# A hybrid attention and delta-rule layer: the scan's output products issued as two column halves

## The chip, the cores and the metric

The kernel runs on one core of one Trainium2 chip. The metric is device time in microseconds (us), the median of the runs shown. A second source is one execution taken with the hardware profiler; its times within the span (from the first to the last instruction) are what the views of the profile give.

## The reference, cut to what matters

The layer takes 256 latent tokens and 256 context tokens of width 2048 and has two branches, multi-head latent attention and a gated DeltaNet with 8 heads, which are projected, gated, summed and followed by a gated MLP. The change lies in the DeltaNet's scan: tokens in chunks of 64, one scan forward and one backward (each with its own decay and gates), first over the four context chunks, whose outputs are not needed, then over the four latent chunks. One step of the reference, per head and direction:

```python
    def step(s, inp):
        u_c, w_c, k_c, g_c = inp[:4]
        v_new = u_c - jnp.einsum('bhcd,bhde->bhce', w_c, s)
        s_next = s * g_c + jnp.einsum('bhcd,bhce->bhde', k_c, v_new)
        if not with_out:
            return s_next, None
        q_c, a_c = inp[4:]
        o = jnp.einsum('bhcd,bhde->bhce', q_c, s) + jnp.einsum('bhcj,bhje->bhce', a_c, v_new)
        return s_next, o
```

The change concerns `o`: the state read by the queries, plus the chunk's attention applied to the new values. Channels are 128 per head.

## The kernel before, in words

Everything before and after the scan is large projections. Each weight matrix comes from memory as fp32 (`raw`, tiles of 128 x 1024, five buffers), is split into a rounded high part `whi` (ScalarE) and a rest `wlo` (VectorE), six buffers of 512 columns each, and TensorE multiplies both: `whi` with 512 moving columns (high and low part of the activations), `wlo` with 256. These are the `fps`, `dps`, `gtp`, `brp` and other groups of the profile; all of them are issued by a helper, so all TensorE rows have line L68 and are told apart by tile names. The weights are stationary: 128 x 128 at a time. A product of plain fp32 operands shows in the profile as two matmuls with a weight load each; here each of the two is called a pass.

The scan is a generator (`scan`, below). It goes through eight steps in the order `steps`, four of the context and then four of the latents (`lat`). Both directions are handled at once: the 64 tokens of the forward chunk lie on partitions 0 to 63 and those of the backward chunk on 64 to 127, and the state `S` has for each head a tile of 128 channels by 128 for each direction. A step does in turn:

- `kp` (from the second step on): keys by state, for each head and direction, into one half of the partitions of a PSUM tile (`kps[h // 4][hs, h % 4]`), so with 64 stationary columns; then VectorE makes the right-hand sides `r`.
- after a yield, `yp`: the solved triangular system by `r`; ScalarE copies it to `y`.
- after another yield, in latent steps, for the two halves `q` of four heads: the outputs `op` (changed here), and in all steps but the last the state update: `sp_`, keys by `y`, from one half of the rows per direction, added to `S` by VectorE (copied by ScalarE in the first step). In `op`, `y` (stationary) is multiplied with `av` for both directions at once, 128 moving columns; then for each direction `S` (stationary) with `qe`, 64 moving columns, is added. The 128 output channels lie on PSUM's partitions.
- ScalarE (steps with `st < 2`) or VectorE copies or adds `op` into `o`.

At each yield the loop around the scan lets a side generator (`fill`) issue projections, the gates `gtp` (`wgd`) and the attention branch's output `brp` (`womla`), and another (`ada`) issue reductions of a conditioning matrix (`rawa`, VectorE, L279). TensorE's order there is pinned to the order of the program; the order on VectorE, SP's DMA queue and the rest comes from a scheduler that weighs the costs of instructions.

The loads of a latent step, `av` (from `As`, L1247) and `qe` (L1249), go into single buffers, so they wait in SP's queue for the `op` of the step before, and loads queued behind them wait too.

Of the kernel before, what the change touches and what calls it, by code (L numbers as in the profile page):

```python
# [53 lines left out]
def hybrid_block(ctx: ExitStack, tc: tile.TileContext, io, dbg=None):  # L54
# [20 lines left out]
    pe, oact, odve = (Ordered(e) for e in (nc.tensor, nc.scalar, nc.vector))  # L75
# [4 lines left out]
    def pool_(name, bufs, side="left"):  # L80
        return tc.tile_pool(name=name, bufs=bufs, side=side, reuse_waits="tile")
# [402 lines left out]
    for k in range(KD):  # L484

        p, late = k // 2 + 1, k % 2 and k + 1 < KD and (k + 1) // 2 in SCP
# [726 lines left out]
    def scan():  # L1213
        pS = ExitStack()
        ps1 = pS.enter_context(pool_("scan", 1, "right"))
        jit = ps1.tile([P, 9, 1024], F32, name="jit")
        TTv = [jit[:, 6 + n].rearrange("p (h c) -> p h c", c=P) for n in range(3)]
        for n in range(3):
            pool.memset(jit[:, 6 + n], 0.0)
        S = ps1.tile([P, HEADS, 2, P], F32, name="S")  # L1220
        steps = (4, 5, 6, 7, 0, 1, 2, 3)

        def load_kv(n):
            kt, v = (jit[:, 2 * j + n % 2].rearrange("p (h c) -> p h c", c=P) for j in (0, 2))
            sync.dma_start(kt, KTs[steps[n]])
            sync.dma_start(v, Vs[steps[n]])
            return kt, v

        def load_system(n):
            st, tt = steps[n], TTv[n % 2]  # L1230
            for d in range(2):
                for r, c, x in ((0, 0, Xq[1]), (32, 32, Xq[2]), (0, 32, Xo)):
                    rs, cs = slice(64 * d + r, 64 * d + r + 32), slice(64 * d + c, 64 * d + c + 32)
                    n = 16 * d + 2 * st
                    sync.dma_start(tt[rs, :, cs], x[n : n + 2].rearrange("a g c i -> c (a g) i"))
            return tt

        def load_ke(n):
            ke = jit[:, 2 + n % 2].rearrange("p (h c) -> p h c", c=P)
            sync.dma_start(ke, KEs[steps[n]])  # L1240
            return ke

        def load_out(st):
            av = TTv[2]
            for d in range(2):
                hs = slice(64 * d, 64 * d + 64)
                sync.dma_start(av[hs, :, hs], As[st, hs])  # L1247
            qe = ps1.tile([P, HEADS, P], F32, tag="qe", name="qe")
            sync.dma_start(qe, QEs[st])  # L1249
            return av, qe  # L1250


        kv, tt, ke = load_kv(0), load_system(0), load_ke(0)
        yield 0
        for n, st in enumerate(steps):
            kt, v = kv
            lat, first, last = st < 4, n == 0, n == 7
            if lat:
                av, qe = load_out(st)
            if n and not last:  # L1260
                ke = load_ke(n)
            if first:
                rs = [v[:, 4 * q : 4 * q + 4] for q in range(2)]
            else:
                rs = [ps1.tile([P, 4, P], F32, tag="r", name="r", bufs=2) for _ in range(2)]
                kps = [psa.tile([P, 4, P], F32, tag="aux", name="kp") for _ in range(2)]

                for h in range(HEADS):
                    for d in range(2):
                        hs = slice(64 * d, 64 * d + 64)  # L1270
                        pe.matmul(kps[h // 4][hs, h % 4], kt[:, h, hs], S[:, h, d], start=True, stop=True)
                for h in range(HEADS):
                    dve.scalar_tensor_tensor(out=rs[h // 4][:, h % 4], in0=kps[h // 4][:, h % 4], scalar=negc[:, st, h : h + 1], in1=v[:, h], op0=ALU.mult, op1=ALU.add)
            if not last:
                kv = load_kv(n + 1)
            yield CA
            y = ps1.tile([P, HEADS, P], F32, tag="y", name="y")
            for q in range(2):
                h4 = slice(4 * q, 4 * q + 4)
                yp = psa.tile([P, 4, P], F32, tag="aux", name="yp")  # L1280
                for j in range(4):
                    pe.matmul(yp[:, j], tt[:, 4 * q + j], rs[q][:, j], start=True, stop=True)
                act.copy(y[:, h4], yp)
            if not last:
                tt = load_system(n + 1)
            yield CB
            if lat:
                op = [psm.tile([P, 4, 2, 64], F32, tag="mm", name="op") for q in range(2)]
            for q in range(2):
                h4 = slice(4 * q, 4 * q + 4)  # L1290
                if lat:
                    for j in range(4):
                        h = 4 * q + j
                        pe.matmul(op[q][:, j].rearrange("p d i -> p (d i)"), y[:, h], av[:, h], start=True, stop=False)
                        for d in range(2):
                            pe.matmul(op[q][:, j, d], S[:, h, d], qe[:, h, 64 * d : 64 * d + 64], start=False, stop=d == 1)
                if not last:
                    for d in range(2):
                        hs = slice(64 * d, 64 * d + 64)
                        sp = psa.tile([P, 4, P], F32, tag="aux", name="sp_")  # L1300
                        for j in range(4):
                            pe.matmul(sp[:, j], ke[hs, 4 * q + j], y[hs, 4 * q + j], start=True, stop=True)
                        if first:
                            act.copy(S[:, h4, d], sp)
                        else:
                            for j in range(4):
                                h = 4 * q + j
                                dve.scalar_tensor_tensor(out=S[:, h, d], in0=S[:, h, d], scalar=gend[:, d, st, h : h + 1],
                                                         in1=sp[:, j], op0=ALU.mult, op1=ALU.add)
            if lat:  # L1310
                for d in range(2):
                    c = st if d == 0 else 3 - st
                    for q in range(2):
                        dst = o[:, 4 * q : 4 * q + 4, 64 * c : 64 * c + 64]
                        src = op[q][:, :, d] if d == 0 else op[q][:, :, d, ::-1]
                        if st < 2:
                            act.copy(dst, src)
                        else:
                            dve.tensor_tensor(out=dst, in0=src, in1=dst, op=ALU.add)
            yield CC  # L1320
        pS.close()
# [36 lines left out]
    for c in scan():  # L1358
        fill(RE * c)
        ada(ADS * c)  # L1360
# [92 lines left out]
    for f in range(NFF):  # L1453
# [12 lines left out]
        y = pf2.tile([P, T], F32, tag="fy", name="fy")  # L1466
# [127 lines left out]
```

## Time and profile before

| what | us |
|---|---|
| runs of the kernel before: median (lowest to highest) of 3 | 1819.82 (1819.18 to 1824.96) |
| the profiled execution, its own time | 1832.12 |
| its span | 1830.3 |
| mean granted TensorE clock of the span | 0.981 |
| TensorE matmul busy | 1775.4 (97%) |
| stretch with the four latent steps' output products | about 835.6 to 942.6 of the span |

How to read the views: PE is TensorE's matmuls and PEld its weight loads, DVE is VectorE, ACT ScalarE, SP the engine that issues most DMAs (SPq its queue). A row of a group has the line, the engine, the operation, the tiles written and read, the shape, and durations in ns (lowest, median, highest). `128*64` at a matmul or weight load is stationary rows by columns; `128x128` behind it is what moves (or, at a load, what is loaded). A row in order of time has the start in us, the time from there to the end of the merged instructions, their number, and in brackets the idle time before it and what ended it. A matmul's duration holds a fixed latency as well, so successive matmuls overlap in these rows; what one costs is read from start to start. The granted clock is given as a share of full speed.

### The profile page before, as it was taken

What the parts mean: (1) busy time and instruction counts of PE and PEld (TensorE: products, weight loads), DVE (VectorE), ACT (ScalarE), POOL (GpSimd) and SP (SyncE); (2) the same over time, 40 slices, a digit from 0 to 9 for tenths busy, and PEclk for the clock granted to TensorE, in tenths of its full rate; (3) what the DMA queues carried; (4) which work ended last, traced back from release to release, by engine and by line L of the source; (5) the groups of instructions that cost most, each with busy time, mean ns of one, the idle gap of its engine ahead of it and who ended that gap; (6) DMA issues with size and microseconds to landing.
All of it is one profiled execution on the core that took longest, in us unless ns stands there. A gap on an engine that the chain in (4) does not pass through costs nothing.

```text
span 1830.3 us, 33168 instructions
## 1 busy us (share of the span) xinstructions
PE 1775.4 (97%) x12509; PEld 1539.3 (84%) x12509; DVE 1365.9 (75%) x2764; ACT 916.8 (50%) x1866; POOL 46.1 (3%) x50
## 2 busy tenths in 40 slices
PE   7999999999999999998999998999999999999999
PEld 6797887887888888788888887888888888888888
DVE  4787899778777786775569988888778888755554
ACT  3345444444666665332346555555555555544443
POOL 0000001000000000000000000000000000000000
PEclk9999999999999999997999998999999999999999
DMA  9973788765777777886665885777666776666664
GB/s 387 410 297 96 215 233 229 218 202 139 228 244 250 234 232 241 301 284 214 214 210 182 296 302 178 257 230 239 191 214 221 224 237 225 187 194 196 201 199 123
DMA packets 195009, 419.72 MB, mean 229 GB/s; under 512 B 61280, under 2 KB 101344, under 8 KB 192416
## 3 DMA queue, kind: packets, MB, share of 16 engines
q1 hardware_dynamic: 167664, 402.37, 67.4%
q10 hardware_dynamic: 27184, 15.23, 2.7%
q8 instruction: 98, 1.61, 0.4%
q14 instruction: 63, 0.52, 0.1%
HBM read 388.57 MB, written 28.84 MB: 228 GB/s over the span
## 4 chain that ended last, share of the span: by engine, by line
PE 60%; issue 9%; DVE 3%; DMA 2%; ACT 1%; POOL 0%; POOLq 0%; ACTq 0%; DVEq 0%
PE fps L68 26%; PE dps L68 13%; PE gtp L68 10%; PE brp L68 2%; DMA rawa<-in_wada 2%; PE op L68 1%; PE vps L68 1%; DVE wlo L122 1%; PE kps L68 1%; PE qps L68 1%; PE yp L68 1%; PE ivp L68 1%; PE sps L68 1%; PE kp L68 1%; PE yps L68 0%
## 5 line engine op out<-in xcount | busy, mean ns | idle before, releaser
L122 DVE TENSOR_TENSOR wlo<-raw,whi 128x512 fp32r<-128x512 f32 (+1 forms) x940 | 632.5, 685 | 206.2 <-ACT whi L121 195.8
L121 ACT CAST whi<-raw 128x512 fp32r<-128x512 f32 (+1 forms) x940 | 572.5, 619 | 409.9 <-PE dps L68 113.7
L68 PE MATMUL fps<-H,whi 128*128 128x512 f32 x1376 | 474.4, 393 | 1.7 <-DVE H L1431 1.7
L68 PE MATMUL fps<-H,wlo 128*128 128x256 f32 x1376 | 372.0, 280 | 0.1
L68 PEld LDWEIGHTS fps<-H,whi 128*128 128x128 f32 x1376 | 253.4, 189 | 53.0 <-issue 2.0
L68 PEld LDWEIGHTS fps<-H,wlo 128*128 128x128 f32 x1376 | 259.5, 189 | 7.6 <-DVE wlo L122 0.5
L68 PE MATMUL gtp<-h,whi 128*128 128x512 f32 x640 | 237.6, 407 | 4.6 <-ACT whi L121 4.6
L68 PE MATMUL mmp<-h,whi 128*128 128x512 f32 x640 | 228.1, 399 | 0.0
L68 PE MATMUL dps<-GB,whi 128*128 128x512 f32 (+1 forms) x595 | 195.7, 378 | 0.0
L68 PE MATMUL gtp<-h,wlo 128*128 128x256 f32 x640 | 177.4, 287 | 5.5 <-DVE wlo L122 5.4
L279 DVE CUSTOM_DVE_ANT_0 rawa<-rawa,sch 128x1024 f32<-128x1024 f32 x128 | 155.8, 1220 | 34.6 <-DMA rawa<-in_wada 32.4
L68 PE MATMUL mmp<-h,wlo 128*128 128x256 f32 x640 | 176.6, 282 | 0.6 <-DVE wlo L122 0.6
L68 PE MATMUL dps<-GB,wlo 128*128 128x256 f32 x560 | 154.1, 280 | 0.0
L68 PEld LDWEIGHTS gtp<-h,whi 128*128 128x128 f32 x640 | 123.4, 194 | 30.8 <-ACT whi L121 5.8
L68 PEld LDWEIGHTS mmp<-h,whi 128*128 128x128 f32 x640 | 119.6, 189 | 25.1 <-issue 0.7
L68 PEld LDWEIGHTS gtp<-h,wlo 128*128 128x128 f32 x640 | 124.1, 194 | 13.4 <-DVE wlo L122 9.0
L68 PEld LDWEIGHTS dps<-GB,whi 128*128 128x128 f32 x595 | 109.2, 188 | 21.2
L68 PEld LDWEIGHTS mmp<-h,wlo 128*128 128x128 f32 x640 | 120.9, 189 | 4.0 <-DVE wlo L122 1.4
L68 PEld LDWEIGHTS dps<-GB,wlo 128*128 128x128 f32 x560 | 105.1, 188 | 0.6
L68 PE MATMUL fp<-h,gh 128*128 128x256 f32 (+1 forms) x448 | 84.2, 288 | 2.7 <-ACT h L68 1.7
L68 PEld LDWEIGHTS fp<-h,gh 128*128 128x128 f32 (+1 forms) x448 | 68.7, 187 | 7.7 <-issue 4.1
L517 ACT COPY fx<-fps 128x256 f32<-128x256 f32 x86 | 31.8, 373 | 66.0 <-PE fps L68 66.0
(565 smaller groups left out, 2584.8 us busy)
## 6 DMA issues: line engine op xcount, KB each, us to landing
rawa<-in_wada SPq DMA_DIRECT2D x128, 512.0 KB, 4.6
raw<-in_wgate SPq DMA_DIRECT2D x82, 512.0 KB, 4.5
raw<-in_wval SPq DMA_DIRECT2D x82, 512.0 KB, 4.7
raw<-in_wdown SPq DMA_DIRECT2D x80, 512.0 KB, 4.3
wt<-in_wadas SPq DMA_DIRECT2D x16, 1024.0 KB, 10.9
raw<-in_wadab SPq DMA_DIRECT2D x32, 512.0 KB, 9.3
raw<-in_wgm SPq DMA_DIRECT2D x32, 512.0 KB, 4.9
raw<-in_wgd SPq DMA_DIRECT2D x32, 512.0 KB, 5.6
```

Of the source, the lines that this page charges most:

```text
L68: i = f(*a, **k)
L121: act.copy(hi, raw)
L122: dve.tensor_tensor(out=lo, in0=raw, in1=hi, op=ALU.subtract)
L279: dve.tensor_tensor_reduce(out=w, in0=w, in1=sch, scale=1.0, scalar=0.0, op0=ALU.mult, op1=ALU.add, accum_out=parts[:, h, j : j + 1])
L517: act.copy(out, ps[:M, T:])
```

## The change

Each product of `op` is issued twice: with the first 64 columns of the stationary tile (channels 0 to 63) into PSUM partitions 0 to 63 and with the last 64 into partitions 64 to 127. What moves is the same for both halves. The arithmetic is the same.

```diff
-                        pe.matmul(op[q][:, j].rearrange("p d i -> p (d i)"), y[:, h], av[:, h], start=True, stop=False)
+                        for m in (slice(0, 64), slice(64, 128)):
+                            pe.matmul(op[q][m, j].rearrange("p d i -> p (d i)"), y[:, h, m], av[:, h], start=True, stop=False)
                         for d in range(2):
-                            pe.matmul(op[q][:, j, d], S[:, h, d], qe[:, h, 64 * d : 64 * d + 64], start=False, stop=d == 1)
+                            for m in (slice(0, 64), slice(64, 128)):
+                                pe.matmul(op[q][m, j, d], S[:, h, d, m], qe[:, h, 64 * d : 64 * d + 64], start=False, stop=d == 1)
```

There are 32 products of `y` and 64 of `S` in the four latent steps; they become 64 and 128, and 192 passes become 384.

On TensorE, at the first latent step, before (the output shape is given here; `op` is the PSUM tile of outputs, `sp_` the state update's, `jit` holds `av`):

```order
L68 MATMUL gtp<-h_314,wlo 128x256
L68 MATMUL op<-jit,y 128x128
L68 MATMUL op<-qe,S 128x64 x2
...
L68 MATMUL sp__10016<-y,jit 128x128 x4
L68 MATMUL sp__10025<-y,jit 128x128 x4
```

and with the change:

```order
L68 MATMUL gtp<-h_314,wlo 128x256
L68 MATMUL op<-jit,y 64x128 x2
L68 MATMUL op<-qe,S 64x64 x4
...
L68 MATMUL sp__10028<-y,jit 128x128 x4
L68 MATMUL sp__10037<-y,jit 128x128 x4
```

The rows of a head come four times in each. Nothing else on TensorE moves. On VectorE, at the state updates of the first latent step, before (`wlo` is a weight's rest, `rawa` the conditioning matrix, `S` the state):

```order
L1308 SCALAR_TENSOR_TENSOR S<-S,dec,sp__10025 128x128 x4
L122 TENSOR_TENSOR wlo<-raw,whi 128x512 x2
L1308 SCALAR_TENSOR_TENSOR S<-S,dec,sp__10046 128x128 x4
L1308 SCALAR_TENSOR_TENSOR S<-S,dec,sp__10055 128x128 x4
L279 ISA rawa,parts<-rawa,sch 128x1024
L279 ISA parts 128x1
```

and with the change:

```order
L1310 SCALAR_TENSOR_TENSOR S<-S,dec,sp__10037 128x128 x4
L122 TENSOR_TENSOR wlo<-raw,whi 128x512 x2
L279 ISA rawa,parts<-rawa,sch 128x1024
L279 ISA parts 128x1
L1310 SCALAR_TENSOR_TENSOR S<-S,dec,sp__10070 128x128 x4
L1310 SCALAR_TENSOR_TENSOR S<-S,dec,sp__10079 128x128 x4
```

One reduction of `rawa` now stands ahead of the second half's updates of `S` instead of behind them. The same happens with one or two reductions or splits in the later latent steps, and in SP's queue one load of `wgd` weights goes ahead of the last latent step's `av` and `qe`. ScalarE and GpSimd keep their order.

## The prediction

> **What bounds the kernel now.** I read the page first: the span, the busy shares and the chain that ended last.
>
> ```profile
> span 1830.3 us, 33168 instructions
> ...
> PE 1775.4 (97%) x12509; PEld 1539.3 (84%) x12509; DVE 1365.9 (75%) x2764; ACT 916.8 (50%) x1866; POOL 46.1 (3%) x50
> ...
> PE 60%; issue 9%; DVE 3%; DMA 2%; ACT 1%; POOL 0%; POOLq 0%; ACTq 0%; DVEq 0%
> PE fps L68 26%; PE dps L68 13%; PE gtp L68 10%; PE brp L68 2%; DMA rawa<-in_wada 2%; PE op L68 1%; PE vps L68 1%; DVE wlo L122 1%; PE kps L68 1%; PE qps L68 1%; PE yp L68 1%; PE ivp L68 1%; PE sps L68 1%; PE kp L68 1%; PE yps L68 0%
> ```
>
> TensorE (PE) is the engine, and `op`, the tile that the change touches, is 1% of the chain. That is small but it is PE time with nothing beside it. The chain of the scan's second half, in order of time, shows the blocks:
>
> ```profile
> 835.89 5.01 PE op L68 x24
> ...
> 843.93 5.31 PE op L68 x24
> ...
> 881.11 2.62 PE op L68 x24
> ...
> 937.43 5.31 PE op L68 x48
> ```
>
> Each `x24` is one half (four heads) of a latent step; in the last step, which has no state update, both halves stand together. The first step's blocks take twice as long as the second's. The table by stretches says why (columns: PE, weight loads, VectorE, ScalarE, POOL, then the granted clock and the DMA share):
>
> ```profile
> 832.20:835.60 3.40, 1.91 (x9) 1.25 (x9) 2.70 (x5) 2.45 (x5) 0.00 (x0) 1.00 0.96 381
> 835.60:852.30 16.70, 16.70 (x83) 16.02 (x81) 6.08 (x18) 2.33 (x6) 0.00 (x0) 0.50 0.32 101
> 880.90:890.00 9.10, 9.10 (x82) 8.68 (x82) 6.03 (x17) 2.70 (x7) 0.00 (x0) 1.00 0.42 156
> ...
> 937.20:942.60 5.40, 5.40 (x51) 5.40 (x49) 1.56 (x4) 1.34 (x3) 0.00 (x0) 1.00 0.48 148
> ```
>
> In all of them PE is busy throughout while VectorE, ScalarE and DMA are half idle. After a stretch in which PE had work for 1.91 of 3.40 us the granted clock fell to 0.50 and stayed there through the whole first step.
>
> **What one head costs now.** A head of `op` is one product of `y` with `av` (128 moving columns) and two of `S` with `qe` (64 each); each fp32 product is recorded as two passes, so 6 passes a head. Successive heads in the first and second latent step, then the last step's start and the instruction behind it:
>
> ```profile
> 836.86 0.74 PE L68 MATMUL op<-jit,y 128*128 128x128 f32 x2
> ...
> 838.14 0.74 PE L68 MATMUL op<-jit,y 128*128 128x128 f32 x2
> ...
> 881.57 0.44 PE L68 MATMUL op<-jit,y 128*128 128x128 f32 x2
> ...
> 882.24 0.44 PE L68 MATMUL op<-jit,y 128*128 128x128 f32 x2
> ```
> ```profile
> 937.27 0.39 PE L68 MATMUL op<-jit,y 128*128 128x128 f32 x2
> ...
> 942.55 0.47 PE L68 MATMUL gtp<-h,whi 128*128 128x512 f32 x1
> ```
>
> A head takes 0.67 us at full clock and 1.28 at half; 5.28 us for 48 passes is 0.11 a pass. The passes differ in moving columns but not in their spacing, so it is the weight load that sets it:
>
> ```profile
> L68 PEld LDWEIGHTS op<-qe,S x128: 190/192/338, 835.9 to 942.4; 128*128 128x128 f32 x128
> L68 PE MATMUL op<-qe,S x128: 222/275/421, 836.1 to 942.5; 128*128 128x64 f32 x128
> L68 PEld LDWEIGHTS op<-jit,y x64: 186/192/335, 835.6 to 942.0; 128*128 128x128 f32 x64
> L68 PE MATMUL op<-jit,y x64: 271/328/580, 835.7 to 942.1; 128*128 128x128 f32 x64
> ```
>
> The shortest passes are 222 and 271 ns: 64 moving columns more cost 49 ns. So a narrow pass streams for about 0.05 us and a wide one for 0.10, against 0.11 between weight loads.
>
> **What the change does to it.** The kernel has one product of the new shape already: `kp`, whose 64 weight columns lie on alternating column halves.
>
> ```profile
> L68 PEld LDWEIGHTS kp<-S,jit x224: 132/137/137, 744.4 to 928.1; 128*64 128x64 f32 x112
> L68 PE MATMUL kp<-S,jit x224: 272/273/323, 744.4 to 928.2; 128*64 128x128 f32 x112
> ```
> ```profile
> 743.82 0.28 PE L68 MATMUL brp<-YM,wlo 128*128 128x256 f32 x1
> ...
> 744.17 0.28 PE L68 MATMUL brp<-YM,wlo 128*128 128x256 f32 x1
> 744.38 1.97 PE L68 MATMUL kp<-S,jit 128*64 128x128 f32 x32
> 746.28 0.50 PE L68 MATMUL brp<-YM,whi 128*128 128x512 f32 x1
> 746.61 0.28 PE L68 MATMUL brp<-YM,wlo 128*128 128x256 f32 x1
> ```
>
> Its 32 half passes end 1.97 us after the first starts. Less the first one's 0.32 that is 1.65 for 16 steps of two: 0.11 for the two halves of a wide pass, though one wide pass alone streams for 0.10. So the halves run side by side, each loading its own weights. The load of 64 columns is 55 ns shorter (137 against 192), so it takes about 0.055 us and hides under a wide stream.
>
> Wide product, `y` by `av`: two passes of exactly `kp`'s shape, 2 x 0.11 = 0.22 us for both halves. Before: 0.22. Nothing gained.
>
> Narrow products, `S` by `qe`: four passes, before 4 x 0.11 = 0.45. Now a half streams 0.05 and loads 0.055. No row shows a 64-column pass on a half. Lower bound: the stream alone, 0.05. Upper bound: `kp`'s 0.11. I take 0.058, the load plus the 3 ns by which `op`'s passes exceed their load, since in `op` and `kp` alike the longer of load and stream sets the spacing. 4 x 0.058 = 0.23.
>
> A head comes to 0.45 instead of 0.67 and saves 0.22; at half clock, by the ratio 1.28/0.67, 0.86 instead of 1.28, saving 0.42. At the bounds a head is 0.42 or 0.66.
>
> Steps two to four: 24 heads x 0.22 = 5.28 us. Step one at half clock: 8 x 0.42 = 3.36. Together 8.64.
>
> **What it adds.** [...] Around `kp`, from the `wlo` pass at 744.17 to the one at 746.61 are 2.44 us; less 0.35 for a pair of fill passes (743.82 to 744.17) and 16 x 0.11 = 1.76, 0.33 is left for both changes: about 0.14 in, since the first pass lacks its early load, and 0.19 out. Steps one to three enter once more (the exit to the row-halved `sp_` exists already): 3 x 0.14, double in the half clock, 0.56. Step four enters and leaves: 0.33. Together 0.9. [...]
>
> Sum: 8.64 - 0.9 = 7.7 us. Against the profiled execution that is 1832.1 to 1824.4 us. The median of the runs is 12.3 us below the profiled time; the removed work is the same in both, so I carry the microseconds over: 1819.8 - 7.7 = 1812.1.
>
> **Who waits.** The loads of the next step wait in SP's queue for `op`, with weight loads queued behind them:
>
> ```profile
> SPq L1247 <- PE op L68: 28.6, 3, 12.2
> ```
>
> A shorter `op` opens that queue earlier by the same amount, so the supply of weights moves with PE. VectorE's state updates wait for PE too, and here the scheduler moves something. In the first step it runs one `rawa` reduction ahead of the second half's updates:
>
> ```profile
> 851.28 1.12 DVE L1308 SCALAR_TENSOR_TENSOR S<-S,dec,sp__10046 128x128 f32<-128x128 f32 x4 [4.97 <-PE sp__10046 L68]
> ...
> 853.35 1.22 DVE L279 CUSTOM_DVE_ANT_0 rawa<-rawa,sch 128x1024 f32<-128x1024 f32 x1
> ```
>
> VectorE stood idle for 4.97 us there, so the 1.22 us fits, and I cost it at nothing. If its data were late, the updates and then `kp` would wait; the reduction at 853.35 shows no wait for its data. What is late next is the fill's weights behind `kp`, where PE waits already:
>
> ```profile
> 865.28 0.39 PE L68 MATMUL gtp<-h,wlo 128*128 128x256 f32 x1 [1.74 <-DVE wlo L122]
> ```
>
> That wait hangs on VectorE, which does the `r` of `kp` first; it moves with `kp`.
>
> **The rivals.** *The clock comes back early* (0.20). The first step's op passes stream only 2 x 0.10 + 4 x 0.05 = 0.4 of 0.67 us. The next rows, in steps of 3.41 us, show that the clock returned after the first stretch of nothing but wide fill:
>
> ```profile
> 849.30:852.71 3.41, 3.41 (x17) 3.17 (x18) 1.43 (x6) 0.62 (x2) 0.00 (x0) 0.50 0.76 208
> 852.71:856.13 3.42, 3.42 (x12) 2.86 (x11) 3.02 (x7) 0.00 (x0) 0.00 (x0) 0.50 1.01 362
> 856.13:859.50 3.37, 3.37 (x21) 2.98 (x20) 0.42 (x1) 0.54 (x2) 0.00 (x0) 1.00 1.00 385
> ```
>
> With 0.4 of 0.45 us streamed the new `op` may be dense enough. Then the block of 16.7 us has 3.4 at half clock, worth 1.7 at full, and the rest of 9.1 - 1.6 = 7.5 at full: 3.4 + 5.8 = 9.2. That saves 7.5 there instead of 3.1, and the time is 1807.7. [...]
>
> *Every pass needs its own place in the issue* (0.14). `kp`'s 0.055 per half pass would then be a price per instruction, whatever its columns: 12 x 0.055 = 0.66 a head, no gain, and the 0.9 of switching is paid: about 1820. Against it, the one-column passes on 32-column strips:
>
> ```profile
> 951.08 0.43 PE L68 MATMUL osp<-ones,osq 128*32 128x1 f32 x32
> ```
>
> 32 of them end within 0.43 us, so issue can do 0.013 or better; but that burst is short. [...]
>
> *The gain is given back to the weight supply* (0.10): steps one to three end in waits like that at 865.28. If they grow by what PE saves, step four alone gains: 8 x 0.22 - 0.33 = 1.4, so 1818.4.
>
> *Slower: the halves queue up* (0.05). If accumulating `op` three products deep kept the halves from overlapping, a head would be 4 x 0.11 + 8 x 0.058 = 0.90; +0.23 for 24 heads, twice nearly that for 8, plus 0.9 gives 1830. It is slower by 0.3% from 0.79 a head. `kp` speaks against it: its two halves share a PSUM tile as well.
>
> **The numbers.** The forecast has 0.48: 1812.1, with the narrow pass's bounds 1810.9 to 1820, and about 1.7 us either way per 3.41 us stretch that falls into the half clock or out of it. 0.03 is left for what I don't see. A measurement here can tell about 0.3% (5.5 us) from no change, so faster means below 1814.4. Faster: 0.43 of the forecast and the early clock's 0.20, 0.63. Same: 0.05 of the forecast, 0.14, 0.10 and 0.01: 0.30. Slower: 0.05 and 0.02: 0.07. The range reaches from the early clock less one stretch and the lower bound, 1805, to no gain, 1820.5; it leaves out the queueing halves and the tails, under 0.2.
>
> **What would show it.** Right: `op` weight loads near 137 ns; heads 0.45 apart in the later steps; the last block 5.28 down to about 3.9; `wlo` waits no longer than now. Wrong: heads at 0.65 (issue) or 0.9 (queueing); blocks short but waits behind them longer (given back); the clock at 1.00 inside the first block (early clock).

## The result, and the profile after

The changed kernel takes 1814.2 us (median of 20 runs, 1805.8 to 1821.0) against 1821.3 (20 runs, 1814.4 to 1833.2): a ratio of 0.996, 95% interval 0.9945 to 0.9974, so 4.7 to 10 us of the 1821. A second comparison (below, e8) gives 0.9971, interval 0.9949 to 0.9994, so 1.1 to 9.3 us; its medians lie 3.6 us apart (1816.1 against 1819.6). The sign is clear in both, the size only to within some us. The forecast was a ratio of 1812.1/1819.8 = 0.9958.

The page of the changed kernel, its span and busy shares:

```profile
span 1810.3 us, 33551 instructions
...
PE 1754.9 (97%) x12701; PEld 1520.6 (84%) x12701; DVE 1366.4 (75%) x2764; ACT 918.4 (51%) x1866; POOL 46.1 (3%) x50
```

TensorE has 192 more matmuls and is 20.5 us less busy. That is more than the timed runs gained; the two profiled executions differ by more than the change, as will be seen. The chain in order of time, at the blocks shown before:

```profile
836.42 1.96 PE op L68 x48
...
840.01 1.96 PE op L68 x48
...
869.19 1.96 PE op L68 x48
...
922.42 3.76 PE op L68 x96
```

Each block of four heads is now 1.96 us, in the first step too, and the last one 3.76. The table by stretches: the idle time ahead of the first step, the first step's block (op, `sp_`, op, `sp_`), the second's, and the last outputs:

```profile
832.90:836.30 3.40, 1.91 (x9) 1.21 (x8) 2.82 (x5) 2.45 (x5) 0.00 (x0) 1.00 0.99 393
836.30:843.60 7.30, 7.30 (x131) 6.87 (x129) 5.69 (x15) 2.33 (x6) 0.00 (x0) 1.00 0.49 159
869.10:876.40 7.30, 7.30 (x130) 6.90 (x129) 6.90 (x19) 2.70 (x7) 0.00 (x0) 1.00 0.70 266
...
922.30:926.20 3.90, 3.90 (x98) 3.79 (x97) 1.45 (x3) 1.34 (x3) 0.00 (x0) 1.00 0.48 134
```

The same 1.91 us of work in 3.40 stood ahead of the first step, but this time the clock stayed at 1.00. The windows are cut a little wider than the blocks: by the start of `op` and of the fill behind the last `sp_`, the second step's block is 7.19 us (869.12 to 876.31) where it was 8.82 (880.95 to 889.77). The passes themselves:

```profile
L68 PEld LDWEIGHTS op<-qe,S x256: 137/138/138, 836.5 to 925.9; 128*64 128x64 f32 x128
L68 PE MATMUL op<-qe,S x256: 219/222/222, 836.6 to 926.0; 128*64 128x64 f32 x128
L68 PEld LDWEIGHTS op<-jit,y x128: 132/138/138, 836.3 to 925.6; 128*64 128x64 f32 x128
L68 PE MATMUL op<-jit,y x128: 272/274/323, 836.4 to 925.7; 128*64 128x128 f32 x128
```

The weight load is 138 ns instead of 192, and the narrow pass's median is 222 ns, which was its lowest before (the median was 275); I read that as a pass that no longer waits for its weights. Two heads in order of time show the spacing:

```profile
836.85 0.39 PE L68 MATMUL op<-jit,y 128*64 128x128 f32 x4
837.07 0.40 PE L68 MATMUL op<-qe,S 128*64 128x64 f32 x8
837.30 0.39 PE L68 MATMUL op<-jit,y 128*64 128x128 f32 x4
```

The wide product takes 0.22 us, the two narrow ones 0.23, the head 0.45. What waits for TensorE got its results sooner, and what TensorE waits for is as before. In the waits of SP's queue and of PE over the latent steps:

```profile
SPq L1247 <- PE op L68: 16.1, 3, 6.0
```
```profile
PE gtp L68 <- DVE wlo L122: 2.7, 4, 1.7
```

SP's wait for `op` fell from 28.6 to 16.1 us. About half of that goes with the long half clock of the profile before: in e10 and e8, two profiles further down with a short half clock in the first step, it is 23.1 before and 17.4 with the change. The waits of `gtp` for its weights in the kernel before, over the same steps, are the same to the digit, and so are the three other rows of TensorE's waits there (1.9, 1.3 and 0.2 us):

```profile
PE gtp L68 <- DVE wlo L122: 2.7, 4, 1.7
```

### The profile page after: what moved, and what is told of

Its sections match the earlier page's. It is cut to its first block, busy times and chain, and to the rows that moved or that the text cites. A ratio compares the mean times of both kernels' runs of the same rounds, so it can differ in the third digit from the quotient of the medians.

```text
span 1810.3 us, 33551 instructions
## 1 busy us (share of the span) xinstructions
PE 1754.9 (97%) x12701; PEld 1520.6 (84%) x12701; DVE 1366.4 (75%) x2764; ACT 918.4 (51%) x1866; POOL 46.1 (3%) x50
## 4 chain that ended last, share of the span: by engine, by line
PE 75%; issue 9%; DMA 8%; DVE 6%; ACT 2%; POOL 1%; SPq 0%; POOLq 0%; ACTq 0%; DVEq 0%
PE fps L68 25%; PE dps L68 13%; PE mmp L68 11%; PE gtp L68 8%; PE fp L68 4%; DMA rawa<-in_wada 3%; PE brp L68 2%; DVE wlo L122 2%; DMA raw<-in_wadab 1%; PE amp L68 1%; PE vps L68 1%; PE op L68 1%; PE tp L68 1%; DVE rawa L279 1%; PE kps L68 1%
## 5 line engine op out<-in xcount | busy, mean ns | idle before, releaser
L68 PE MATMUL gtp<-h,whi 128*128 128x512 f32 x640 | 232.5, 400 | 5.0 <-ACT whi L121 5.0
```

What stands on the lines that cost most here:

```text
L68: i = f(*a, **k)
```

## The experiments

**Which products gain** (e1, e2). e1 halves the narrow products alone, behind the four whole wide ones; e2 the wide ones alone. Both leave out the addition of the two, so their results are not the layer's; they serve for the time alone. A change of mode, here and below, is TensorE's going from whole stationary tiles to halves or back.

```diff
 # e1, against the change
+                    for j in range(4):
+                        pe.matmul(op[q][:, j].rearrange("p d i -> p (d i)"), y[:, 4 * q + j], av[:, 4 * q + j], start=True, stop=True)
                     for j in range(4):
                         h = 4 * q + j
-                        for m in (slice(0, 64), slice(64, 128)):
-                            pe.matmul(op[q][m, j].rearrange("p d i -> p (d i)"), y[:, h, m], av[:, h], start=True, stop=False)
...
-                                pe.matmul(op[q][m, j, d], S[:, h, d, m], qe[:, h, 64 * d : 64 * d + 64], start=False, stop=d == 1)
+                                pe.matmul(op[q][m, j, d], S[:, h, d, m], qe[:, h, 64 * d : 64 * d + 64], start=True, stop=True)
```

```diff
 # e2, against the change
                     for j in range(4):
-                        h = 4 * q + j
                         for m in (slice(0, 64), slice(64, 128)):
-                            pe.matmul(op[q][m, j].rearrange("p d i -> p (d i)"), y[:, h, m], av[:, h], start=True, stop=False)
+                            pe.matmul(op[q][m, j].rearrange("p d i -> p (d i)"), y[:, 4 * q + j, m], av[:, 4 * q + j], start=True, stop=True)
+                    for j in range(4):
+                        h = 4 * q + j
...
-                            for m in (slice(0, 64), slice(64, 128)):
-                                pe.matmul(op[q][m, j, d], S[:, h, d, m], qe[:, h, 64 * d : 64 * d + 64], start=False, stop=d == 1)
+                            pe.matmul(op[q][:, j, d], S[:, h, d], qe[:, h, 64 * d : 64 * d + 64], start=True, stop=True)
```

> Only the narrow products (states by queries) are issued as halves; the four wide ones of a block stand whole ahead of them. The narrow products overwrite the wide ones' sums here, which leaves out the addition of the two. Theory (each half loads and streams by itself, the longer of the two sets the spacing): the wide products gain nothing from halving, so a block of four heads takes as long as with the full change, 4 x 0.22 + 4 x 0.23 + 0.14 = about 1.95 us in the first three latent steps; the last step has one change of mode more, 3.76 + 0.33 = about 4.1 us. Time 1814 to 1815 on the scale of the change's 1814.2. Rival (the halved wide products carry the gain): blocks of about 2.7 us and the time of the kernel before.

> Only the wide products are issued as halves, four heads of them ahead of the whole narrow ones, which overwrite them (the addition of the two is left out). Theory: wide 4 x 0.22, narrow 4 x 0.45, a change of mode in and out 0.33: blocks of about 3.0 us at full clock against 2.72 to 2.82 before; slower than the kernel before by about 1.5 to 2 us, within noise. Rival (the wide halves carry the gain): blocks of about 2.0 us and a gain like the full change's.

The chains in order of time, of e1:

```profile
865.41 1.97 PE op L68 x40
...
869.02 2.17 PE op L68 x40
...
919.11 4.14 PE op L68 x80
```

and of e2:

```profile
870.15 2.95 PE op L68 x32
...
874.75 2.95 PE op L68 x32
...
927.38 5.91 PE op L68 x64
```

e1's blocks are 2.0 to 2.2 us, near the change's 1.96, and its ratio to the kernel before is 0.997 (0.9946 to 0.9994). e2's are 2.95 against 2.62 to 2.82 before, its ratio 1.0017 (0.9995 to 1.0038), not told apart from 1; one of its twelve runs took 6041 us and is not in the ratio. The whole gain lies on the narrow products; the halved wide ones only spare a change of mode.

**What a change of mode costs** (e3). The wide product of each head stays whole.

```diff
 # e3, against the change
-                        for m in (slice(0, 64), slice(64, 128)):
-                            pe.matmul(op[q][m, j].rearrange("p d i -> p (d i)"), y[:, h, m], av[:, h], start=True, stop=False)
+                        pe.matmul(op[q][:, j].rearrange("p d i -> p (d i)"), y[:, h], av[:, h], start=True, stop=False)
```

> As the change, but the wide product of each head stays whole, so that TensorE goes from whole to halves and back in every head; the arithmetic is complete. Theory with a drain at each change of mode: 0.22 + 0.23 + 0.33 = 0.78 us a head, blocks of about 3.1 us, the last step about 6.2; slower than the kernel before by 3 to 4 us. Rival (a change of mode costs nothing by itself): 0.45 a head, blocks of 1.9 us, as fast as the full change.

Heads of e3 in order of time:

```profile
837.61 0.49 PE L68 MATMUL op<-jit,y 128*128 128x128 f32 x2
838.03 0.45 PE L68 MATMUL op<-qe,S 128*64 128x64 f32 x8
838.41 0.49 PE L68 MATMUL op<-jit,y 128*128 128x128 f32 x2
```

A head is 0.80 us, 0.35 more than with the change, for one exit and one entry. So a pair of mode changes costs 0.35 us here (what TensorE does in that time no run shows; the drain of the expectation was my reading), and a mixture within the head eats the gain: 0.80 us is more than the 0.67 of the kernel before. The ratio to that kernel is 1.0025 (0.9998 to 1.0052); the 3 to 4 us expected are within that interval, but so is no difference.

**Halves again** (e4): four strips of 32 channels.

```diff
-                        for m in (slice(0, 64), slice(64, 128)):
+                        for m in [slice(32 * s, 32 * s + 32) for s in range(4)]:
...
-                            for m in (slice(0, 64), slice(64, 128)):
+                            for m in [slice(32 * s, 32 * s + 32) for s in range(4)]:
```

> The change with four strips of 32 channels instead of two halves of 64; the arithmetic is complete. Theory: the four strips stream side by side, wide 0.10 to 0.11 and narrow 0.05 to 0.06 us for all four, the loads are shorter still and hidden: blocks of 1.9 to 1.96 us, no gain over the two halves. Rival (passes are issued one by one, no faster than the 0.02 us of the densest long run of the kernel before): 16 narrow passes a head take 0.33 instead of 0.23, blocks of about 2.35 us, and a third of the gain is lost.

The rows of `op` in e4 and the place of one block where it stopped:

```profile
L68 PEld LDWEIGHTS op<-qe,S x512: 106/110/111, 834.9 to 923.7; 128*32 128x32 f32 x171
L68 PE MATMUL op<-qe,S x512: 218/219/243, 835.1 to 923.7; 128*32 128x64 f32 x171
```
```profile
838.82 0.40 PE L68 MATMUL op<-jit,y 128*32 128x128 f32 x8
839.04 0.41 PE L68 MATMUL op<-qe,S 128*32 128x64 f32 x16
839.26 0.40 PE L68 MATMUL op<-jit,y 128*32 128x128 f32 x8
839.48 0.40 PE L68 MATMUL op<-qe,S 128*32 128x64 f32 x15
840.75 0.24 PE L68 MATMUL op<-qe,S 128*32 128x64 f32 x1 [0.87 <-issue]
```

16 narrow passes take 0.22 us, 14 ns each, so passes have no price of their own near 0.02 us, and the rival falls. The load is shorter again (110 ns) and gains next to nothing, 0.01 us a narrow group, as it should if the stream, 0.05 us by the estimate from the 222 and 271 ns of before, is by then the longer of the two. Four of the six single blocks take 1.90 us (the last step's double one 3.67). The other two stopped for 0.87 and 1.20 us with nothing that the profile shows to wait for. The ratio is 0.9968 (0.9943 to 0.9993), that of the change.

**The clock** (e5, e6). Nine copies of `y` onto itself hold TensorE idle ahead of the outputs, in the kernel before (e5) and in the changed one (e6). Each ran once, in 1891.6 and 1852.7 us.

```diff
             if lat:
+                for _ in range(9):
+                    oact.copy(y, y)
                 op = [psm.tile([P, 4, 2, 64], F32, tag="mm", name="op") for q in range(2)]
```

> The kernel before with nine copies of y onto itself on ScalarE ahead of the outputs of each latent step, so that TensorE stands idle for some us before them; the arithmetic is complete. Both theories: the idle time halves the clock in most latent steps, and the block of outputs and state updates (op, sp_, op, sp_) then takes about 16 us at 0.50 and the clock returns only with the fill behind it, as in the first latent step of the kernel before.

> The same idle time, with the change's halves. Theory of the forecast (the clock stays down until the fill): a block takes 4 x 3.6 to 3.8 us or so, about 13.4 us at 0.50. Rival (early clock: the denser op counts as busy): the clock is back at 1.00 within one or two stretches of 3.41 us and the block takes 9 to 11 us.

e5, the first two latent steps' blocks, the fill behind the first, and what follows:

```profile
848.30:864.90 16.60, 16.60 (x80) 15.95 (x80) 4.78 (x15) 1.81 (x5) 0.00 (x0) 0.50 0.26 71
896.90:913.50 16.60, 16.60 (x80) 15.96 (x80) 4.16 (x14) 1.29 (x4) 0.00 (x0) 0.50 0.37 130
864.90:869.50 4.60, 4.60 (x15) 3.89 (x15) 1.97 (x6) 0.62 (x1) 0.00 (x0) 0.50 0.93 275
869.50:873.00 3.50, 3.50 (x22) 3.07 (x21) 1.68 (x3) 1.90 (x4) 0.00 (x0) 0.99 0.85 336
```

e6, the first latent step in two parts, then the second's and the third's block:

```profile
845.20:849.30 4.10, 4.05 (x50) 3.97 (x51) 0.69 (x1) 0.96 (x3) 0.00 (x0) 0.50 0.75 241
849.30:854.30 5.00, 5.00 (x80) 4.71 (x79) 3.72 (x12) 0.95 (x4) 0.00 (x0) 0.99 0.05 11
884.20:892.60 8.40, 8.40 (x128) 8.05 (x128) 3.71 (x12) 1.29 (x4) 0.00 (x0) 0.84 0.64 242
922.10:933.60 11.50, 11.50 (x129) 10.97 (x129) 4.20 (x15) 0.00 (x0) 0.00 (x0) 0.60 0.03 8
```

With whole products the block stays at 0.50 for 16.6 us and the clock returns only with the fill. With halves the blocks take 9.1, 8.4 and 11.5 us. The clock is back 4.1 us after the first `op` pass in the first step, 2.7 in the second and 4.1 in the last, but only after 9.2 us in the third: there the mean of 0.60 over 11.5 us, between 0.50 and 1.00, leaves 9.2 us at half clock. In that step it missed the first half's 3.7 us of `op`, stayed down through the `sp_` passes and came back within the second half's. So the early-clock rival is right that halved `op` can bring the clock back before the fill, though not always at once (one block lies above its 9 to 11 us), and the forecast's price for a step at half clock (13.4 us) was reached in none.

**How often the first step runs at half clock** (e8 to e11): the two kernels profiled again.

> The change itself once more, on the same chip as the three kernels beside it, for its blocks and its clock in a second profile. Theory: blocks of 1.96 us in the first three latent steps and 3.76 in the last wherever the clock is 1.00, with or without the half clock in the first step; 6 to 8 us faster than the kernel before. Rival (the gain of the first comparison was the clock's luck): no difference from the kernel before here.

> The kernel before, unchanged, for a second profile of its clock. Reading A: the half clock of about 20 us in the first latent step is what usually happens, so the step's block (op, sp_, op, sp_) takes about 16 us. Reading B: it is one execution's luck, and the block takes about 9 us at full clock. By A the change should gain about 12 us, by B about 6.4.

> As the run beside it: the kernel before, for a third profile. A: the first latent step's block about 16 us at 0.50; B: about 9 us.

> As the two runs beside it: the kernel before, for a fourth profile. A: the first latent step's block about 16 us at 0.50; B: about 9 us.

The chain of the first two blocks in e9 (first latent step), e10 and e11:

```profile
836.74 3.31 PE op L68 x24
841.68 2.82 PE op L68 x24
```
```profile
831.45 3.60 PE op L68 x24
836.69 2.82 PE op L68 x24
```
```profile
839.83 5.01 PE op L68 x24
847.87 5.31 PE op L68 x24
```

e11 is like the first profile of before (1837.5 and 1832.1 us), reading A of the expectation. In e9 and e10 (1825.0 and 1814.7 us) the half clock ends within the first block, near reading B. In e9 it lasted from about 834.6 to 838.0 us and `op` began at 836.5, in e10 from 830.0 to 833.4 with `op` from 831.3, with dense fill between; in e11 and the first profile the fall and `op` came together, at 839.6 and at 835.7. So it seems to hang on what stands in the 3.4 us that begin with the fall; four executions don't prove it.

The timed runs say more about how often. Their granted clock over the span was 0.981 and 0.982 in the two profiles with the long half clock, and 0.987 to 0.992 in e9, e10, e8 and the first profile of the change. Of 53 timed runs of the kernel before that were taken beside e1 to e11, five lie at 0.980 or 0.981 and the next at 0.986; of the change's 32, none lies below 0.986. If that low clock marks the long half clock, and no trace of those runs was kept to confirm it, it comes in about one execution of the kernel before in ten.

The chain of e8, the change once more, and the clock in its first block:

```profile
837.39 3.28 PE op L68 x48
842.31 1.95 PE op L68 x48
```
```profile
837.30:840.20 2.90, 2.90 (x41) 2.89 (x42) 1.31 (x4) 0.00 (x0) 0.00 (x0) 0.51 0.87 292
840.20:845.80 5.60, 5.60 (x92) 5.25 (x88) 4.01 (x11) 2.33 (x6) 0.00 (x0) 1.00 0.16 51
```

Here the half clock came at about 836.8 us, `op` followed from 837.3, and the clock was back at 840.2, 3.4 us after its fall. e8's ratio is the 0.9971 given above, with 1816.1 us. The 6 to 8 us expected of it lie inside its interval of 1.1 to 9.3, but its medians moved only 3.6.

**A further step** (e7): the same thought on the state update, whose products lie on row halves.

```diff
-                    for d in range(2):
-                        hs = slice(64 * d, 64 * d + 64)
-                        sp = psa.tile([P, 4, P], F32, tag="aux", name="sp_")
-                        for j in range(4):
-                            pe.matmul(sp[:, j], ke[hs, 4 * q + j], y[hs, 4 * q + j], start=True, stop=True)
+                    sps = [psa.tile([P, 4, P], F32, tag="aux", name="sp_") for d in range(2)]
+                    for j in range(4):
+                        for d in range(2):
+                            hs = slice(64 * d, 64 * d + 64)
+                            pe.matmul(sps[d][:, j], ke[hs, 4 * q + j], y[hs, 4 * q + j], start=True, stop=True)
+                    for d in range(2):
+                        sp = sps[d]
```

> The change, and the state update's products issued in turn for the two directions, so that the two row halves of TensorE have work at the same time; the arithmetic is complete. Theory (halves of any kind run side by side, each with its own loads): a state update of 16 passes takes 8 x 0.11 + 0.3 = about 1.2 us instead of 1.64; 14 of them save about 6 us: 1808 on the scale of the change's 1814.2. Rival (the halves overlap well enough already, or the wait behind the update takes it): no difference from the change.

In order of time, the first passes of an update in e7, then its first two latent blocks:

```profile
833.94 0.37 PE L68 MATMUL sp__10070<-y,jit 64*128 64x128 f32 x1
833.95 0.37 PE L68 MATMUL sp__10071<-y,jit 64*128 64x128 f32 x1
834.16 0.27 PE L68 MATMUL sp__10070<-y,jit 64*128 64x128 f32 x1
```
```profile
828.90:835.00 6.10, 6.10 (x129) 5.72 (x128) 4.49 (x14) 2.33 (x6) 0.00 (x0) 1.00 0.56 194
860.60:866.70 6.10, 6.10 (x130) 5.72 (x129) 5.49 (x15) 2.70 (x7) 0.00 (x0) 1.00 0.56 225
```

Both directions run from the first pass on; a block with two updates is 6.09 us from start to start (828.94 to 835.03) instead of 7.19, so an update fell by 0.55 from about 1.63. The time is 1806.5 us, a ratio of 0.9924 to the kernel before (0.9895 to 0.9954), beside 1816.1 us and 0.9971 for the change on the same chip. Fourteen updates at 0.55 make 7.7 of the 9.6 us between those medians; the rest was not traced.

## Why the prediction was right, point by point

- *The bound.* TensorE alone, with no cover: right. The blocks shrank, and what follows them moved up.
- *The price of a pass.* For the two halves of a pass together: narrow 0.058 taken, (0.23/4) 0.0575 measured; wide 0.11, unchanged; head 0.45, measured 0.45. (Read from `kp`, 1.65 us over 16 steps is 0.103 and not 0.11; the change's own wide halves gave 0.11.) e1 and e2 show that the narrow products carry it all. What I took to lie behind it, the longer of load and stream per half, is an estimate from the loads and pass lengths of before; it fits e4 too, where a still shorter load (110 ns) gained next to nothing (0.22 us a narrow group instead of 0.23).
- *The change of mode.* 0.33 a pair taken, 0.35 from e3. The last step's outputs: about 3.9 forecast, 3.76 measured.
- *The first step at half clock.* This term failed. I took the one profile of before as the rule and priced both kernels as staying at 0.50 through the block: 8 x 0.42 = 3.36 us. Of four profiles of the kernel before, two had the long half clock and two a short one, and by the granted clock of the timed runs the long one is rarer still; with the halves the clock returned early (e8, and three of e6's four steps) or did not fall there at all (the profile after). At full clock throughout, the blocks of both profiles give 3 x (2.72 + 2.82) + 5.28 = 21.9 us before (the first step taken like the second, a block from its start to the next instruction) and 3 x 3.92 + 3.76 = 15.5 after: 6.4 us. The forecast's own terms at full clock come to 32 x 0.22 = 7.04 less the 0.75 of 3 x 0.14 + 0.33, so 6.3. The medians moved by 7.0, and 3.6 in the second comparison. The other 1.4 us of the 7.7 price a state that no profile of the change shows; that the total stays near 7.0 with them in it is luck. In an execution where the kernel before keeps the half clock and the change does not, the clock adds up to 5.7 us (an estimate: the rival's 12.1 less 6.4); where both have a short one or none, about nothing. (The 16.7 and 9.1 us taken for the blocks are lengths of windows; the blocks are 16.5 and 8.8.)
- *The rivals.* Issue: refuted by the narrow halves, two in 0.0575 and so 0.029 each where it needs 0.055, and by e4's 14 ns. Given back: refuted by the waits, equal to the digit. Queueing halves: refuted by the head of 0.45. Early clock: borne out in e8, where the half clock lasted about 3.4 us, and in three of e6's four steps; its time of 1807.7 was not reached, and it too supposed the long half clock in every run of before.
- *VectorE's moved reduction.* With the blocks shorter it has less idle time to lie in, yet TensorE's waits did not grow: no cost shows. No run put the old order back to separate it.

## What to carry to other kernels

Where TensorE's stationary loads set the spacing (here fp32 weights of 128 columns, 192 ns a load and 0.11 us a pass under 64 moving ones), issue the product as two column halves: here a load fell to 138 ns and the two halves of a pass took 0.0575 us together, while loads of 110 ns in e4 gained only 0.01 us more a narrow group. Keep halves together, since each pair of mode changes cost 0.35 us here, and let products for different halves follow one another rather than come in runs, which took 0.55 us off an update of about 1.63 in e7. Before a term rests on a clock that fell, profile the same kernel two or three times, and read the granted clock of the timed runs too.

## What the runs showed of the hardware

A TensorE that is busy by the records need not win its clock back. At 0.50, 16.6 us of whole `op` and `sp_` passes, with weight loads nearly throughout (15.95 us), did not bring it back in e5; the halved ones did 2.7 to 4.1 us after their start in three of e6's four steps, and after 9.2 us in the other. Wide fill did too: in e5 it began at 864.9 and the clock was back at about 869.5. By the estimates from the rows of before, whole `op` streams 0.4 of 0.67 us and halved `op` 0.4 of 0.45. Which share suffices was not measured.

Row halves overlapped only as far as the order let them: eight passes of one half ahead of eight of the other took about 1.63 us (838.38 to 840.01 in the chain after), in turn 0.55 less (7.19 to 6.09 for two, in e7).

The holes of 0.87 and 1.20 us in e4, of four strips and twice as many passes as the change, stay unexplained. They were not tried further.
